# Down projections of an encoder trunk: the seven weight products interleaved, and a weight's three forms spread over three steps

## The chip, the cores and the metric

The kernel runs on one core of a Trainium2 chip, as one program and one launch. The metric is the device time of a whole execution in microseconds (us), lower is better; several executions are timed and the median counts. TensorE (PE) multiplies, VectorE (DVE), ScalarE (ACT) and GpSimd (POOL) do the element work, and SyncE (SP) and POOL start transfers from HBM into SBUF. PE's results go to PSUM.

## The reference

Two layers over 512 tokens of width 1024, in float32. Each layer has two feed-forward blocks (SwiGLU, hidden width 2816) with attention between them and a small embedding gate behind them:

```python
def swiglu(x, w_gate, w_up, w_down):
    return (jax.nn.silu(x @ w_gate) * (x @ w_up)) @ w_down
...
h += 0.5 * SwiGLU_1(RMSNorm(h))
...
h += 0.5 * SwiGLU_2(RMSNorm(h))
```

So there are four feed-forward blocks, and the change is in the last product of each, `@ w_down`: 512 tokens x 2816 times 2816 x 1024.

## The kernel before

*Number format.* PE multiplies float32 as split numbers: each operand is cut into a high part (a copy on ACT, L148, in `split`) and a low part (source minus high part, on DVE, L149), and every product is three matmuls, high x high, high x low, low x high. In `product` these are the lines L452, L453 and L454.

*Feed-forward block* (`ffn`). A loop over 22 pairs of hidden chunks computes gate and up projections (`pair_front`, `pair`, `pair_fast`) and leaves the activations a[0] to a[21], 128 hidden rows by 512 tokens each. Then `down` computes the projection.

*Down projection* (`down`). It is a 2 x 2 block product with seven products in place of eight (a Strassen-Winograd form). Hidden rows are halved, a[k] and a[K2 + k] with K2 = 11; tokens are halved, `l` and `r`; the weight has the four quarters b11, b12, b21 and b22, 11 chunks of 128 x 512 each. A *unit* is two chunks of a quarter, 128 x 1024 or 512 KB; there are six units, the last of one chunk. The seven products accumulate in PSUM over the six units and use these weights and activations:

| product | weight | activation | PSUM |
|---|---|---|---|
| r1, first half | b11 | x1, left | mm |
| r3, first half | b11 + b12 | x1, right | sc |
| r2 | b21 | x2, left | mm, ob |
| rb | b12 + b22 | x3, left | tr |
| r1, second half | b12 + b22 + b11 | x3, right | mm |
| rc | b12 + b22 + b11 + b21 | x2, right | mm, ob |
| r3, second half | b22 | x4 | sc |

x1 to x4 are the split parts of a[k] or a[K2 + k] after subtractions and additions on POOL (L467, L489, L490, L492). x1 takes the right half of a[k] less that of a[K2 + k].

*Weights.* `load` (L439) brings a unit by SP's queue into one of five raw buffers `wr`. `add` (L443) lays another quarter's unit onto the same buffer by an accumulating transfer on POOL's queue. `parts` splits the buffer into `wh` (ACT) and `wl` (DVE), of which there are four each. A raw buffer thus goes through as many as four forms; an add may start only when the split of the form before it has read the buffer, and the next split only when the add has landed.

*Order.* The statements are written out product by product. A scheduler reorders them somewhat before the program is fixed; after that each engine takes its instructions in a fixed order, and each queue its transfers. In the kernel before there are three loops over the units (called loop 1, 2 and 3 below), then r3's second half (a fourth), in which the x4 parts are made, and a tail: transposes on PE (L520), then 0.5 times the result plus the stream `kept` (L524), the next norm's scaling and split (`norm_split`, L211 and L212) and its squares (L224).

Of the kernel before, what the change touches and what calls it, by code (L numbers as in the profile page):

```python
# [20 lines left out]
NF = DFF // P  # L21
# [15 lines left out]
K2 = NF // 2  # L37
# [9 lines left out]
class Trunk:  # L47
# [353 lines left out]
    def ffn(self, i, which, k_next):  # L401


        nc, io = self.nc, self.io
        gu, dn = io[f"gu{which}"], io[f"dn{which}"]
        first = i == 0 and which == 1
        a, y, t = [], [None] * KC, [None] * (KC // 2)

        kept = io["xT"].rearrange("p c t -> c p t") if first else self.put_away()
        for m in range(NF):  # L410
# [11 lines left out]
        self.down(dn[i], a, kept)  # L422

    def down(self, w, a, kept):

        nc, H = self.nc, T // 2
        l, r = slice(0, H), slice(H, T)
        self.kept = self.dp.tile([KC, P, T], F32, name=self.nm("kept"))  # L430
        copy, tt, sub = nc.scalar.activation, nc.vector.tensor_tensor, ALU.subtract
        pool = nc.gpsimd.tensor_tensor
        b11, b12, b21, b22 = (w[n] for n in range(4))
        units = [slice(u, min(u + 2, K2)) for u in range(0, K2, 2)]
        ks = lambda u: range(u.start, u.stop)

        def load(b, u):
            raw = self.wr.tile([P, UNIT], F32, tag="wr", name=self.nm("wr"))[:, :(u.stop - u.start) * T]
            nc.sync.dma_start(raw, b[:, u.start * T:u.stop * T])  # L439
            return raw  # L440

        def add(raw, b, u):
            nc.gpsimd.dma_start(raw, b[:, u.start * T:u.stop * T], accum_op=ALU.add)  # L443

        def product(out, u, ws, xs, cols, start, stop):
            mm = nc.tensor.matmul
            for j, k in enumerate(ks(u)):
                wh, wl = (x[:, j * T:(j + 1) * T] for x in ws)
                for i, p in enumerate(out):
                    c = slice(cols.start + i * P, cols.start + (i + 1) * P)  # L450
                    xh, xl = (x[:, c] for x in xs[k])
                    mm(p, xh, wh, start=start and k == 0, stop=False, skip_group_check=True)  # L452
                    mm(p, xh, wl, start=False, stop=False, skip_group_check=True)  # L453
                    mm(p, xl, wh, start=False, stop=stop and k == K2 - 1, skip_group_check=True)  # L454
# [8 lines left out]
        x1, x2, x3, x4 = ([None] * K2 for _ in range(4))  # L463
        for u in units:
            raw = load(b11, u)
            for k in ks(u):
                pool(a[k][:, r], a[k][:, r], a[K2 + k][:, r], op=sub)  # L467
# [12 lines left out]
        for o, p in zip(c1, r2):  # L480
            tt(o, p, o, op=ALU.add)
        c11 = c1

        rb, rc = [self.tbank(), self.tbank()], [self.bank(), self.obank()]
        for u in units:
            raw = load(b12, u)
            add(raw, b22, u)
            for k in ks(u):
                pool(a[k][:, r], a[k][:, r], a[k][:, l], op=sub)  # L489
                pool(a[k][:, l], a[k][:, r], a[K2 + k][:, r], op=ALU.add)  # L490
                x3[k] = self.split_chunk(a[k], nc.vector)
                pool(a[K2 + k][:, l], a[K2 + k][:, l], a[k][:, r], op=ALU.add)  # L492
            product(rb, u, self.parts(raw), x3, l, True, True)
            add(raw, b11, u)
            product(r1, u, self.parts(raw), x3, r, False, True)
            add(raw, b21, u)
            product(rc, u, self.parts(raw), x2, r, True, True)
        c2, c21 = copied(r1), [self.act(), self.act()]
        u3 = [self.act(), self.act()]
        for i in range(2):  # L500
            tt(u3[i], c2[i], rb[i], op=sub)
            tt(c21[i], rc[i], u3[i], op=ALU.add)
            tt(c5[i], c5[i], u3[i], op=sub)
        c22 = c5

        hs = []
        for m in range(KC):
            hs.append(self.act())
            nc.sync.dma_start(hs[m], kept[m])
        for u in units:  # L510
            raw = load(b22, u)
            for k in ks(u):
                hi, lo = self.act(F32R), self.act(F32R)
                self.split(a[K2 + k][:, l], hi[:, l], lo[:, l])
                x4[k] = hi, lo
            product(r3, u, self.parts(raw), x4, l, False, True)

        def turned(out, x, j):
            for i, y in enumerate(x):
                nc.tensor.transpose(out[:, i * P:(i + 1) * P], y[:, j * P:(j + 1) * P], self.ident)  # L520

        def done(m, p, c):
            h = hs[m]
            nc.vector.scalar_tensor_tensor(h[:, c], p, 0.5, h[:, c], op0=ALU.mult, op1=ALU.add)  # L524
# [942 lines left out]
```

## Time and profile before

| | us |
|---|---|
| median of 3 runs (lowest to highest) | 2456.99 (2453.18 to 2458.53) |
| profiled execution, its own time | 2457.63 |
| its span in the trace | 2455.9 |
| PE busy in the span | 2155.1 (88%) |
| DVE, ACT, POOL busy | 1627.9, 1130.8, 487.0 |
| DMA traffic | 339.09 MB, mean 138 GB/s |
| mean granted TensorE clock | 0.932 |

The profile divides the span in 40 slices and shows busy shares of them, groups instructions by line, engine and operation, and names for each group what ended the engine's idle time before it (its releaser). The trace behind it holds every instruction with start and length, which can be listed by engine (a timeline), by source line or by window of time. "DMA share" is the mean busy share of the core's 16 DMA engines. The four down projections begin at 238.1, 982.8, 1488.6 and 2162.8 us.

### The profile page before, as it was taken

The numbers are of one execution on the slowest core, as the hardware profiler recorded it, in microseconds if no ns is written. First come the engines' busy times: TensorE is split into PE (matmuls) and PEld (weight loads), VectorE is DVE, ScalarE is ACT, GpSimd is POOL, SyncE is SP. The second block draws the span as 40 slices with busy tenths as digits, with TensorE's granted clock in tenths as the row PEclk, the third lists the DMA queues.
The fourth block names the chain that finished last, engine by engine and source line by source line (L and its number), as shares of the span: only waits on it lengthen the run. The fifth ranks groups of instructions, "written<-read, shape, count | busy, mean of one in ns | idle before, by whom it ended". The sixth has DMA issues, their size and how long they took to land. (4 is left out here: it accounts for less than half of the span.)

```text
span 2455.9 us, 32981 instructions
## 1 busy us (share of the span) xinstructions
PE 2155.1 (88%) x12294; PEld 1839.0 (75%) x12294; DVE 1627.9 (66%) x2571; ACT 1130.8 (46%) x1902; POOL 487.0 (20%) x534
## 2 busy tenths in 40 slices
PE   9999766899999999676899997767999999976678
PEld 7999444778788999454689995445988899964456
DVE  8788442789767788452777885517777678855175
ACT  5455322467654455231554553414666545534142
POOL 0012320342211011330210114302000101143021
PEclk9999887999999999888899998878999999988789
DMA  6675464554335565474545764646442456646452
GB/s 198 176 184 144 107 133 93 196 97 94 91 87 163 152 181 162 93 150 77 201 146 151 188 173 92 152 85 188 121 112 83 155 158 181 172 88 148 85 185 77
DMA packets 128048, 339.09 MB, mean 138 GB/s; under 512 B 23824, under 2 KB 31504, under 8 KB 127888
## 3 DMA queue, kind: packets, MB, share of 16 engines
q1 hardware_dynamic: 97728, 241.52, 30.6%
q0 software_dynamic: 30016, 95.44, 22.7%
q8 instruction: 96, 1.57, 0.3%
q14 instruction: 64, 0.52, 0.1%
q10 hardware_dynamic: 144, 0.04, 0.0%
HBM read 308.62 MB, written 17.27 MB: 133 GB/s over the span
## 5 line engine op out<-in xcount | busy, mean ns | idle before, releaser
L149 DVE TENSOR_TENSOR wl<-wr,wh 128x1024 fp32r<-128x1024 f32 (+1 forms) x503 | 611.2, 1222 | 504.9 <-ACT wh L148 503.9
L148 ACT ACTIVATE wh<-wr 128x1024 fp32r<-128x1024 f32 (+1 forms) x503 | 511.6, 1028 | 833.6 <-DMA wr<-in_dn_dram 472.2
L372 PE MATMUL mm<-act,wh 128*128 128x256 f32 x1088 | 307.9, 283 | 0.0
L373 PE MATMUL mm<-act,wl 128*128 128x256 f32 x1088 | 307.9, 283 | 0.0
L371 PE MATMUL mm<-act,wh 128*128 128x256 f32 x1088 | 307.9, 283 | 0.0
L173 PE MATMUL mm<-act,wh 128*128 128x512 f32 (+1 forms) x648 | 256.1, 397 | 4.2 <-DVE act L664 2.5
L174 PE MATMUL mm<-act,wh 128*128 128x512 f32 (+1 forms) x648 | 257.0, 397 | 2.5 <-DVE act L212 2.5
L175 PE MATMUL mm<-act,wl 128*128 128x512 f32 (+1 forms) x648 | 256.2, 395 | 3.3 <-DVE wl L149 3.3
L452 PE MATMUL mm<-wh,act 128*128 128x512 f32 x264 | 127.1, 506 | 141.2 <-ACT wh L148 136.2
L371 PEld LDWEIGHTS mm<-act,wh 128*128 128x128 f32 x1088 | 208.9, 192 | 0.2
L372 PEld LDWEIGHTS mm<-act,wh 128*128 128x128 f32 x1088 | 208.9, 192 | 0.2
L373 PEld LDWEIGHTS mm<-act,wl 128*128 128x128 f32 x1088 | 208.9, 192 | 0.0
L452 PEld LDWEIGHTS mm<-wh,act 128*128 128x128 f32 x264 | 58.4, 233 | 181.9 <-ACT wh L148 163.6
L149 DVE TENSOR_TENSOR act<-act,act 128x512 fp32r<-128x512 f32 (+1 forms) x192 | 180.5, 985 | 13.5 <-ACT act L148 13.4
L443 POOL DMA_DIRECT2D wr<-in_dn_dram x96 | 85.2, 888 | 477.5 <-DVE wl L149 449.3
L349 POOL DMA_DIRECT2D wr<-in_gu_dram x68 | 60.0, 882 | 494.6 <-DMA wr<-in_gu_dram 251.8
L371 PE MATMUL sc<-act,wh 128*128 128x256 f32 x544 | 154.0, 283 | 0.0
L372 PE MATMUL sc<-act,wh 128*128 128x256 f32 x544 | 154.0, 283 | 0.0
L373 PE MATMUL sc<-act,wl 128*128 128x256 f32 x544 | 154.0, 283 | 0.0
L174 PEld LDWEIGHTS mm<-act,wh 128*128 128x128 f32 x648 | 123.7, 191 | 27.9 <-DVE act L212 4.8
L173 PEld LDWEIGHTS mm<-act,wh 128*128 128x128 f32 x648 | 123.2, 190 | 27.8 <-issue 2.7
L175 PEld LDWEIGHTS mm<-act,wl 128*128 128x128 f32 x648 | 123.6, 191 | 27.1 <-DVE wl L149 4.7
(232 smaller groups left out, 4998.9 us busy)
## 6 DMA issues: line engine op xcount, KB each, us to landing
wr<-in_gu_dram SPq DMA_DIRECT2D x176, 512.0 KB, 4.4
wr<-in_dn_dram SPq DMA_DIRECT2D x80, 512.0 KB, 3.7
wr<-in_dn_dram POOLq DMA_DIRECT2D x80, 512.0 KB, 5.9
wr<-in_gu_dram POOLq DMA_DIRECT2D x68, 512.0 KB, 5.5
rb<-in_gu_dram SPq DMA_DIRECT2D x68, 256.0 KB, 2.6
act<-kept SPq DMA_DIRECT2D x56, 256.0 KB, 5.3
wr<-in_qk_ab_dram SPq DMA_DIRECT2D x20, 512.0 KB, 3.9
kept<-act POOLq DMA_DIRECT2D x32, 256.0 KB, 4.8
```

The source lines that it names most:

```text
L148: self.put(self.nc.scalar.activation(hi, src, AF.Copy))
L149: self.put((lo_eng or self.nc.vector).tensor_tensor(lo, src, hi.bitcast(F32), op=ALU.subtract))
L173: mm(out, stat[0], mov[0], start=start, stop=False)
L174: mm(out, stat[0], mov[1], start=False, stop=False)
L175: return mm(out, stat[1], mov[0], start=False, stop=stop)
L349: nc.gpsimd.dma_start(rs, w[:, :UNIT], accum_op=ALU.add)
L371: mm(out, w[0][:, c], xs[k][0][:, x], start=start and k == 0, stop=False, skip_group_check=True)
L372: mm(out, w[0][:, c], xs[k][1][:, x], start=False, stop=False, skip_group_check=True)
L373: mm(out, w[1][:, c], xs[k][0][:, x], start=False, stop=stop and k == half - 1, skip_group_check=True)
L443: nc.gpsimd.dma_start(raw, b[:, u.start * T:u.stop * T], accum_op=ALU.add)
L452: mm(p, xh, wh, start=start and k == 0, stop=False, skip_group_check=True)
```

## The change

All of the change is in `ffn` and `down`.

- Loops 1 and 2 become one (loop A): step s has r1 of unit s, the add of b12, r2 of unit s with a raw buffer of its own, and r3 of unit s - 1.
- Loop 3 becomes a loop B of eight steps: step s loads b12 and adds b22 for unit s + 1, then rb of unit s and the add of b11, r1 of unit s - 1 and the add of b21, rc of unit s - 2. The x4 parts of unit s - 2 are made there too, in halves of one tile, and no longer in the loop of r3's second half.
- The first two subtractions and splits of x1 are written ahead of the last gate and up pair (`lead_part`).

The number of matmuls, of splits and of transfers is the same.

```diff
         for m in range(NF):
+            if m == NF - 1:
+                for k in range(2):
+                    self.lead_part(x1, a, k)
...
+    def lead_part(self, x1, a, k):
+        if x1[k] is None:
+            right = slice(T // 2, T)
+            self.nc.gpsimd.tensor_tensor(a[k][:, right], a[k][:, right], a[K2 + k][:, right], op=ALU.subtract)
+            x1[k] = self.split_chunk(a[k], self.nc.vector)
...
-        for u in units:
-            raw = load(b11, u)
-            for k in ks(u):
-                pool(a[k][:, r], a[k][:, r], a[K2 + k][:, r], op=sub)
-                x1[k] = self.split_chunk(a[k], nc.vector)
-            product(r1, u, self.parts(raw), x1, l, True, True)
-            add(raw, b12, u)
-            product(r3, u, self.parts(raw), x1, r, True, True)
-        c1, c5 = copied(r1), copied(r3)
         r2 = [self.bank(), self.obank()]
-        for u in units:
-            raw = load(b21, u)
-            for k in ks(u):
-                x2[k] = self.split_chunk(a[K2 + k], nc.vector)
-            product(r2, u, self.parts(raw), x2, l, True, True)
+        n, raws = len(units), {}
+        for s in range(n + 1):
+            if s < n:
+                u = units[s]
+                raw = raws[s] = load(b11, u)
+                for k in ks(u):
+                    self.lead_part(x1, a, k)
+                product(r1, u, self.parts(raw), x1, l, True, True)
+                add(raw, b12, u)
+                raw = load(b21, u)
+                for k in ks(u):
+                    x2[k] = self.split_chunk(a[K2 + k], nc.vector)
+                product(r2, u, self.parts(raw), x2, l, True, True)
+            if s:
+                u = units[s - 1]
+                product(r3, u, self.parts(raws[s - 1]), x1, r, True, True)
+        c1 = copied(r1)
         for o, p in zip(c1, r2):
             tt(o, p, o, op=ALU.add)
-        c11 = c1
+        c11, c5 = c1, copied(r3)
+
+        def summed(s):
+            raws[s] = load(b12, units[s])
+            add(raws[s], b22, units[s])
 
         rb, rc = [self.tbank(), self.tbank()], [self.bank(), self.obank()]
-        for u in units:
-            raw = load(b12, u)
-            add(raw, b22, u)
-            for k in ks(u):
-                pool(a[k][:, r], a[k][:, r], a[k][:, l], op=sub)
-                pool(a[k][:, l], a[k][:, r], a[K2 + k][:, r], op=ALU.add)
-                x3[k] = self.split_chunk(a[k], nc.vector)
-                pool(a[K2 + k][:, l], a[K2 + k][:, l], a[k][:, r], op=ALU.add)
-            product(rb, u, self.parts(raw), x3, l, True, True)
-            add(raw, b11, u)
-            product(r1, u, self.parts(raw), x3, r, False, True)
-            add(raw, b21, u)
-            product(rc, u, self.parts(raw), x2, r, True, True)
+        summed(0)
+        for s in range(n + 2):
+            if s + 1 < n:
+                summed(s + 1)
+            if s < n:
+                u = units[s]
...
+                product(rb, u, self.parts(raws[s]), x3, l, True, True)
+                add(raws[s], b11, u)
+            if 0 < s <= n:
+                u = units[s - 1]
+                product(r1, u, self.parts(raws[s - 1]), x3, r, False, True)
+                add(raws[s - 1], b21, u)
+            if s > 1:
+                u = units[s - 2]
+                product(rc, u, self.parts(raws[s - 2]), x2, r, True, True)
+                for k in ks(u):
+                    t = self.act(F32R)
+                    x4[k] = t[:, l], t[:, r]
+                    self.split(a[K2 + k][:, l], *x4[k])
...
         for u in units:
             raw = load(b22, u)
-            for k in ks(u):
-                hi, lo = self.act(F32R), self.act(F32R)
-                self.split(a[K2 + k][:, l], hi[:, l], lo[:, l])
-                x4[k] = hi, lo
             product(r3, u, self.parts(raw), x4, l, False, True)
```

Three places show how instructions stand on the engines. In the rows, a name is a tile with its number; the part before the arrow is written, the part behind it read. The lines of the changed kernel are numbered anew: L450 is `load`, L454 `add`, L463 to L465 the matmuls of `product`, L545 the transposes, L549 the sums with the stream.

PE, behind r1's first unit, before (the tiles `mm` are r1's, the tiles `sc` r3's):

```order
L454 MATMUL mm_2759<-wh_2774,act_2771 128x512
L452 MATMUL sc_2760<-wh_2791,act_2765 128x512
L452 MATMUL sc_2761<-wh_2791,act_2765 128x512
L453 MATMUL sc_2760<-wl_2792,act_2765 128x512
L454 MATMUL sc_2760<-wh_2791,act_2766 128x512
```

The same place in the changed kernel (`mm_2772` and `ob_2773` are r2's):

```order
L465 MATMUL mm_2769<-wh_2776,act_2640 128x512
L463 MATMUL mm_2772<-wh_2803,act_2795 128x512
L464 MATMUL mm_2772<-wl_2804,act_2795 128x512
L465 MATMUL mm_2772<-wh_2803,act_2796 128x512
L463 MATMUL ob_2773<-wh_2803,act_2795 128x512
```

Where r3 of the same unit followed r1, r2 of that unit now follows, and then come r1 and r2 of the next unit and r3 of the first.

POOL's transfers in loop 3, before, from the add that is last of its kind ahead of the run of chained ones (a `wr` number names a raw buffer's unit: 3244, 3311, 3378, 3445 and 3512 are units 1 to 5):

```order
L443 DMA wr_3177<-in_dn_dram 128x1024
L443 DMA wr_3244<-in_dn_dram 128x1024
L443 DMA wr_3512<-in_dn_dram 128x512
L443 DMA wr_3244<-in_dn_dram 128x1024
L443 DMA wr_3311<-in_dn_dram 128x1024 x2
L443 DMA wr_3378<-in_dn_dram 128x1024 x2
L443 DMA wr_3445<-in_dn_dram 128x1024 x2
L443 DMA wr_3512<-in_dn_dram 128x512 x2
```

The same queue in loop B of the changed kernel (3177, 3180, 3214, 3265, 3338 and 3411 are units 0 to 5):

```order
L454 DMA wr_3177<-in_dn_dram 128x1024
L454 DMA wr_3180<-in_dn_dram 128x1024
L454 DMA wr_3338<-in_dn_dram 128x1024
L454 DMA wr_3177<-in_dn_dram 128x1024
L454 DMA wr_3214<-in_dn_dram 128x1024
L454 DMA wr_3180<-in_dn_dram 128x1024
L454 DMA wr_3265<-in_dn_dram 128x1024
L454 DMA wr_3411<-in_dn_dram 128x512
L454 DMA wr_3214<-in_dn_dram 128x1024
```

Two adds onto one unit stood next to each other; now those of two or three units alternate.

DVE at the end of the stage, before (L547 takes r3's second half, `sc`, out of PSUM):

```order
L212 SCALAR_TENSOR_TENSOR act_3764<-act_3572,gain,act_3763 128x512
L212 SCALAR_TENSOR_TENSOR act_3778<-act_3574,gain,act_3777 128x512
L149 TENSOR_TENSOR wl_3884<-wr_3882,wh_3883 128x1024
L547 TENSOR_TENSOR act_3554<-sc_2760,act_3554 128x256 x2
L547 TENSOR_TENSOR act_3555<-sc_2761,act_3555 128x256
```

The same place in the changed kernel (L572 takes r3's second half out of PSUM):

```order
L149 TENSOR_TENSOR wl_3873<-wr_3871,wh_3872 128x1024
L572 TENSOR_TENSOR act_3587<-sc_2770,act_3587 128x256 x2
L572 TENSOR_TENSOR act_3588<-sc_2771,act_3588 128x256
L549 SCALAR_TENSOR_TENSOR act_3601<-tr_3719,act_3601 128x512
L549 SCALAR_TENSOR_TENSOR act_3603<-tr_3732,act_3603 128x512
L572 TENSOR_TENSOR act_3588<-sc_2771,act_3588 128x256
L212 SCALAR_TENSOR_TENSOR act_3726<-act_3601,gain,act_3725 128x512
```

The four wide norm scalings of 128 x 512 (and the four sums that feed them) stood ahead of r3's last use; they now stand behind it.

More of the change, by code (lines that the diff above doesn't have):

```diff
@@ L409, in ffn @@
         kept = io["xT"].rearrange("p c t -> c p t") if first else self.put_away()
+        x1 = [None] * K2
         for m in range(NF):
+            if m == NF - 1:
+                for k in range(2):
+                    self.lead_part(x1, a, k)
             if m < FRONT:
@@ L421, in ffn, with down @@
         self.begin_norm(k_next)
-        self.down(dn[i], a, kept)
-    def down(self, w, a, kept):
+        self.down(dn[i], a, x1, kept)
+    def lead_part(self, x1, a, k):
[3 more added lines that the diff above has]
+            x1[k] = self.split_chunk(a[k], self.nc.vector)
+    def down(self, w, a, x1, kept):
         nc, H = self.nc, T // 2
@@ L462, in down @@
         r1, r3 = [self.bank(), self.bank()], [self.sbank(), self.sbank()]
-        x1, x2, x3, x4 = ([None] * K2 for _ in range(4))
-        for u in units:
-            raw = load(b11, u)
-            for k in ks(u):
-                pool(a[k][:, r], a[k][:, r], a[K2 + k][:, r], op=sub)
-                x1[k] = self.split_chunk(a[k], nc.vector)
-            product(r1, u, self.parts(raw), x1, l, True, True)
-            add(raw, b12, u)
-            product(r3, u, self.parts(raw), x1, r, True, True)
@@ L472, in down @@
-        c1, c5 = copied(r1), copied(r3)
-        r2 = [self.bank(), self.obank()]
-        for u in units:
-            raw = load(b21, u)
-            for k in ks(u):
-                x2[k] = self.split_chunk(a[K2 + k], nc.vector)
-            product(r2, u, self.parts(raw), x2, l, True, True)
+        r2 = [self.bank(), self.obank()]
+        x2, x3, x4 = ([None] * K2 for _ in range(3))
+        n, raws = len(units), {}
[14 more added lines that the diff above has]
+                product(r3, u, self.parts(raws[s - 1]), x1, r, True, True)
@@ new lines, in down @@
+        for s in range(n + 2):
[4 more added lines that the diff above has]
+                for k in ks(u):
+                    pool(a[k][:, r], a[k][:, r], a[k][:, l], op=sub)
+                    pool(a[k][:, l], a[k][:, r], a[K2 + k][:, r], op=ALU.add)
+                    x3[k] = self.split_chunk(a[k], nc.vector)
+                    pool(a[K2 + k][:, l], a[K2 + k][:, l], a[k][:, r], op=ALU.add)
+                product(rb, u, self.parts(raws[s]), x3, l, True, True)
[7 more added lines that the diff above has]
+                product(rc, u, self.parts(raws[s - 2]), x2, r, True, True)
+                for k in ks(u):
+                    t = self.act(F32R)
+                    x4[k] = t[:, l], t[:, r]
+                    self.split(a[K2 + k][:, l], *x4[k])
```

## The prediction, made before the changed kernel was run

> **What bounds the kernel now.** I read the page's costliest groups first, for the lines of the diff (a bracketed arrow names what ended an engine's idle time):
>
> ```profile
> L149 DVE TENSOR_TENSOR wl<-wr,wh 128x1024 fp32r<-128x1024 f32 (+1 forms) x503 | 611.2, 1222 | 504.9 <-ACT wh L148 503.9
> L148 ACT ACTIVATE wh<-wr 128x1024 fp32r<-128x1024 f32 (+1 forms) x503 | 511.6, 1028 | 833.6 <-DMA wr<-in_dn_dram 472.2
> L452 PE MATMUL mm<-wh,act 128*128 128x512 f32 x264 | 127.1, 506 | 141.2 <-ACT wh L148 136.2
> L443 POOL DMA_DIRECT2D wr<-in_dn_dram x96 | 85.2, 888 | 477.5 <-DVE wl L149 449.3
> ```
>
> The down projections' matmuls (L452) wait for the weight's high part (ACT), ACT waits for the weight's transfer, and the accumulating transfer (POOL, L443) waits for the low part (DVE): a ring. The windows of the four stages, first r1 matmul to last r3 matmul (length, then busy time of PE, weight load, DVE, ACT, POOL; granted clock; DMA share; GB/s):
>
> ```profile
> 238.10:451.20 213.10, 149.40 (x485) 106.55 (x484) 100.39 (x106) 67.91 (x97) 55.27 (x61) 0.81 0.55 126
> 982.80:1195.50 212.70, 146.92 (x485) 103.62 (x484) 101.08 (x106) 67.79 (x97) 55.80 (x61) 0.82 0.55 126
> 1488.60:1701.30 212.70, 147.51 (x486) 104.07 (x485) 100.33 (x107) 67.93 (x98) 55.34 (x61) 0.83 0.55 126
> 2162.80:2377.00 214.20, 147.89 (x485) 105.03 (x484) 97.82 (x106) 67.87 (x97) 55.23 (x61) 0.82 0.55 126
> ```
>
> They are alike, mean 213.2 us. No engine is full, DMA is at 0.55, and the clock falls to 0.82. Stage one by parts (loops 1 and 2; loop 3; the wait for r3):
>
> ```profile
> 238.00:322.00 84.00, 61.60 (x213) 43.55 (x211) 48.55 (x45) 30.36 (x44) 37.29 (x41) 0.88 0.57 128
> 322.00:425.40 103.40, 66.30 (x188) 46.08 (x188) 29.70 (x32) 23.33 (x28) 12.09 (x15) 0.76 0.47 88
> 425.40:434.20 8.80, 4.60 (x19) 3.13 (x18) 7.71 (x10) 3.23 (x6) 2.16 (x3) 0.50 0.94 308
> ```
>
> The ring in loop 3, on the timelines of POOL and ACT (start, length):
>
> ```profile
> 338.33 0.87 POOL L443 DMA_DIRECT2D wr<-in_dn_dram  x1 [8.48 <-DVE wl L149]
> ...
> 346.54 0.87 POOL L443 DMA_DIRECT2D wr<-in_dn_dram  x1 [5.50 <-DVE wl L149]
> 355.97 0.87 POOL L443 DMA_DIRECT2D wr<-in_dn_dram  x1 [8.57 <-DVE wl L149]
> ```
> ```profile
> 343.93 1.06 ACT L148 ACTIVATE wh<-wr 128x1024 fp32r<-128x1024 f32 x1 [7.34 <-DMA wr<-in_dn_dram]
> 352.23 2.00 ACT L148 ACTIVATE wh<-wr 128x1024 fp32r<-128x1024 f32 x2 [7.25 <-DMA wr<-in_dn_dram]
> ```
>
> One add of the chain every 8.8 us (338.33 to 355.97, halved; the row left out is a unit's first add, fetched ahead): issue, landing and split in a row. Two such adds make a unit, hence some 17.6 us for 36 matmuls.
>
> What PE needs alone, from the last r3 matmuls of stage one:
>
> ```profile
> 447.62 0.39 PE L452 MATMUL sc<-wh,act 128*128 128x512 f32 x1
> ...
> 450.80 0.39 PE L454 MATMUL sc<-wh,act 128*128 128x512 f32 x1
> ```
>
> 15 matmuls start 3.18 us apart from first to last, 0.227 us each: 462 of a stage are 105 us. So 108 us of each stage are waits and cold clock; that is the pot.
>
> **The change part by part.** It adds no matmul, split or transfer; it changes which waits overlap.
>
> *Loop A (r1, r2, r3 interleaved), 198 matmuls, PE floor 45 us.* Between r1(s) and r3(s), which is the add b12's round trip of 8.8 us, PE now has r2(s), r3(s-1), r1(s+1) and r2(s+1): 48 matmuls or 10.9 us. So the trip is covered. DVE and POOL then decide:
>
> ```profile
> 233.00:252.00 19.00, 16.59 (x80) 13.59 (x79) 16.45 (x17) 8.80 (x16) 18.20 (x17) 0.82 0.27 55
> ```
> ```profile
> L467 POOL TENSOR_TENSOR act<-act,act 128x256 f32<-128x256 f32 x44 | 32.2, 733 | 257.9 <-DVE act L398 257.9
> L489 POOL TENSOR_TENSOR act<-act 128x256 f32<-128x256 f32 x44 | 48.7, 1140 | 9.6 <-DVE act L149 9.6
> ```
> ```profile
> 232.64 0.69 DVE L149 TENSOR_TENSOR act<-act,act 128x512 fp32r<-128x512 f32 x1
> ```
> ```profile
> L149 DVE TENSOR_TENSOR act<-act,act 128x512 fp32r<-128x512 f32 x30 | 33.5, 1163 | 2.5 <-ACT act L148 2.5
> ```
>
> In a quiet place a chunk's low part takes 0.69 us on DVE and a POOL operation 0.73; side by side (the mean of stage one, the mean of L489) 1.16 and 1.14. A pair takes 1.17 us where one after the other would be 1.42: side by side is 1.21 times as fast as in turn. Loop A's DVE work: three products' weights, 3 x (5 x 1.22 + 0.69) = 20.4, and 31 chunk parts (9 of x1, 11 of x2, 11 of x3, which run early as in the kernel before) x 0.69 = 21.4, together 41.8. POOL: two late subtractions and 22 for x3, 24 x 0.73 = 17.5. (41.8 + 17.5) / 1.21 = 49 us. ACT has at most 39 splits x 1.03 = 40. I take **49** for loop A; ends 45 (PE alone) and 59 (DVE and POOL strictly in turn). Before: 84.
>
> The Trainium skill ("SBUF — State Buffer", section "SBUF: two separate sides") says that VectorE and GpSimd share a port pair under an exclusive lock, held for a whole instruction, so the loser stands still. It would give the 59; the trace does not bear it out strictly, since 0.69 + 0.73 in turn is more than the 1.17 seen.
>
> *Between the loops.* r1, r2 and r3 end together; the copies of r3 and their POOL and DVE followers hold ACT. Before, the same spot cost:
>
> ```profile
> 327.47 0.80 PE L452 MATMUL mm<-wh,act 128*128 128x512 f32 x1 [5.83 <-ACT wh L148]
> ```
>
> That gap held a whole add, which now is issued one unit ahead. I take **3 + 2** (ends 0 and 5.8): 3 wait, 2 for the cold clock behind it, by these rows:
>
> ```profile
> 268.37 0.73 PE L452 MATMUL sc<-wh,act 128*128 128x512 f32 x2 [1.61 <-ACT wh L148]
> ...
> 269.89 0.39 PE L453 MATMUL sc<-wl,act 128*128 128x512 f32 x1
> ```
> ```profile
> 400.21 1.06 PE L452 MATMUL mm<-wh,act 128*128 128x512 f32 x2 [2.51 <-ACT wh L148]
> ...
> 402.06 0.63 PE L454 MATMUL mm<-wh,act 128*128 128x512 f32 x1
> ```
>
> 1.61 us idle left the matmuls at 0.39 us, 2.51 us left them at 0.63; a dozen cold ones cost about 2 us more. The Trainium skill ("TensorE: Matmul & The Clock Gate", section on HAM oscillation) sets the harmful gap above about 3.4 us; by it the 2 would drop out, 8 us over four stages, but the row at 400.21 speaks against it.
>
> *Loop B (rb of s, r1 of s-1, rc of s-2), 198 matmuls, PE floor 45.* Each add now waits for a split of its own step and is used a step later; between rb(s) and r1(s) PE has 36 matmuls, 8.2 us, against the trip of 8.8. Three adds and one load per step are in flight. Then the 16 DMA engines count. Loop 3's transfers over 98 us (322 to 420):
>
> ```profile
> q0 software_dynamic: 1910, 6.35, 39.5%
> q1 hardware_dynamic: 720, 2.36, 8.3%
> ...
> wr<-in_dn_dram POOLq DMA_DIRECT2D x9, 512.0 KB, 5.6
> ```
>
> Accumulating: 0.395 x 98 / 6.35 = 6.1 us of all engines per MB; plain: 0.083 x 98 / 2.36 = 3.45. Loop B has 18 adds of 8.65 MB and six loads of 2.88 MB: 52.8 + 9.9 = 62.7 us. About 12 us of that (three loads at 1.8, two adds at 3.2) fit into loop A, whose own need is 17.6 for adds and 11 loads less five fetched before the stage, 10.9, or 28.5 of 49 us. 62.7 - 12 + 3 for the last split and its matmuls: **54** (ends 48, PE with its drain, and 66, no head start). That the adds can lie side by side is seen in loop 2 of the kernel before:
>
> ```profile
> 305.44 0.88 POOL L443 DMA_DIRECT2D wr<-in_dn_dram  x1
> ...
> 307.82 0.88 POOL L443 DMA_DIRECT2D wr<-in_dn_dram  x1
> ...
> 310.64 0.88 POOL L443 DMA_DIRECT2D wr<-in_dn_dram  x1 [1.10 <-DVE act L149]
> ```
> ```profile
> 300.00:322.00 22.00, 18.48 (x72) 12.59 (x71) 20.40 (x20) 11.65 (x19) 13.41 (x15) 1.00 0.89 220
> ```
>
> Adds 2.4 and 2.8 us apart, the engines at 0.89. Before: 103.4. The x4 splits now sit in this loop, where ACT and DVE had most of their time idle: no cost (11 x 0.69 = 7.6 us at most, if each delayed a weight).
>
> *r3's second half*, 66 matmuls: **15** (17 with a cold start). Transposes and stream loads that came between (8.8 us, above) now come behind or beside it.
>
> *Tail.* That has a price. Before, the first four chunks' sums (L524) and norms (L212) were over before r3 ended at 451.2:
>
> ```profile
> 430.97 1.34 DVE L524 SCALAR_TENSOR_TENSOR act<-tr,act 128x512 f32<-128x512 f32 x2 [0.38 <-DMA act<-in_xT_dram]
> ```
> ```profile
> 443.70 1.41 DVE L212 SCALAR_TENSOR_TENSOR act<-act,gain,act 128x512 fp32r<-128x512 f32 x2
> ...
> 446.71 1.41 DVE L212 SCALAR_TENSOR_TENSOR act<-act,gain,act 128x512 fp32r<-128x512 f32 x2
> ```
>
> Now all transposes stand behind r3 in PE's order, and 4 x 0.67 + 4 x 0.71 = 5.5 us of DVE follow it, partly under other waits: **5** (ends 2 and 6).
>
> *First parts ahead of the last pair:* two splits, which DVE did inside that pair before as well (232.64): nothing; if PE waited for them, 2 x 0.69 us.
>
> Sum: 49 + 5 + 54 + 15 + 5 = 128 us against 213.2, that is 85 less, times four 341. The profiled execution took 2457.63 (span 2455.9), against a median of 2456.99; 2457.6 - 341 = **2117 us**.
>
> **The rivals.** (1) *DMA as the bound*: no head start in loop B, 66 instead of 54: 2165. For it: 0.89 share in loop 2. Against: 0.55 over the stage. (2) *DVE and POOL in turn* through loop A, 59 or 60: 2159. (3) Both: 2207. (4) *Adds only in pairs*: 9 rounds of 8.8 us and 3 is 82 for loop B, 2229; for it ACT takes splits in order, so a late landing holds the next two. (5) *The other side*: each add still waits for the one before it, since POOL and ACT both take their work in a fixed order. 18 adds x 8.8 = 158 us for loop B, stage 232, 19 more than now: 2533. It turns where an add costs over 7.7 us in series ((213.2 - 74) / 18). Against it are the adds 2.4 us apart. (6) PE's wait merely moves, and nothing is gained.
>
> **How the numbers follow.** Forecast 0.55, (1) 0.17, (2) 0.12, (3) 0.05, (4) 0.05, (5) 0.04, (6) 0.02. If every term falls at its lower end: 45 + 0 + 48 + 15 + 2 = 110, 2045. The range runs from a little above that, 2055, to 2205, holding the forecast, (1) and (2) and leaving (3) to (6) out. A difference within 0.2% could not be told from none here. Faster 0.94, same 0.02, slower 0.04.
>
> **What would show it.** In the new profile: r1, r2, r3 over within 45 to 60 us of a stage's start; POOL's adds in loop B about 3 us apart rather than 8.8; DMA share there above 0.8; granted clock of the stage above 0.95; matmuls waiting for the high part for under 30 us in all instead of 136; L549 and L212 all behind r3. Wrong would be adds still 8 us apart, or a matmul gap at every step.

## The result, and the profile after

The changed kernel takes 2139.85 us (median of 4 runs, 2138.97 to 2141.0) against 2455.35 for the kernel before (four runs now, one more than ahead of the prediction): a ratio of 0.8714, 95% interval 0.8699 to 0.8730. The forecast was 2117 with a range of 2055 to 2205. The profiled execution took 2138.97 (span 2137.2, granted clock 0.981 where it was 0.932).

The four stages in the new trace, again from the first r1 matmul to the last r3 matmul (start:end, length, busy time of PE, weight load, DVE, ACT, POOL; clock; DMA share; GB/s):

```profile
238.70:364.90 126.20, 113.46 (x466) 89.47 (x465) 89.31 (x96) 62.19 (x90) 56.17 (x52) 0.95 0.84 203
900.30:1027.40 127.10, 111.57 (x466) 88.56 (x465) 89.63 (x96) 62.03 (x89) 56.16 (x52) 0.96 0.83 203
1327.70:1454.30 126.60, 113.38 (x466) 89.45 (x465) 88.32 (x94) 61.47 (x89) 56.16 (x52) 0.95 0.83 199
1922.90:2051.00 128.10, 113.47 (x466) 89.95 (x465) 89.81 (x96) 62.18 (x89) 56.21 (x52) 0.93 0.83 201
```

They take 127.0 us in the mean where they took 213.2; over the four stages that is about 345 us less. The span fell by 318.7 only, so 26 us came back outside the stages. The groups by line say what became of the ring:

```profile
L148 ACT ACTIVATE wh<-wr 128x1024 fp32r<-128x1024 f32 (+1 forms) x503 | 516.0, 1029 | 577.7 <-DMA wr<-in_dn_dram 148.5
```
```profile
L454 POOL DMA_DIRECT2D wr<-in_dn_dram x96 | 83.8, 901 | 185.1 <-DVE wl L149 122.2 <-DMA wr<-in_dn_dram 60.5 <-issue 2.4
L463 PE MATMUL sc<-wh,act 128*128 128x512 f32 x176 | 70.9, 403 | 18.9 <-ACT wh L148 18.9
L463 PE MATMUL mm<-wh,act 128*128 128x512 f32 x264 | 103.7, 393 | 0.0
L463 PE MATMUL tr<-wh,act 128*128 128x512 f32 x88 | 40.9, 465 | 17.1 <-ACT act L148 17.1
```

ACT's wait for down weights fell from 472 us to 148, POOL's wait in front of the adds from 477 to 185, and the wait of the first matmuls of a product for a weight's high part from 136 us on `mm` alone to 18.9, all on `sc`. On `tr` (rb's tiles) a new wait of 17.1 us stands, for the high part of an activation. POOL's timeline in loop B of stage one shows the adds (start, length):

```profile
306.37 0.87 POOL L454 DMA_DIRECT2D wr<-in_dn_dram  x1 [3.74 <-DVE wl L149]
308.11 0.87 POOL L454 DMA_DIRECT2D wr<-in_dn_dram  x1 [0.87 <-DVE wl L149]
309.85 0.87 POOL L454 DMA_DIRECT2D wr<-in_dn_dram  x1 [0.87 <-DVE wl L149]
317.12 0.87 POOL L454 DMA_DIRECT2D wr<-in_dn_dram  x1 [6.41 <-DVE wl L149]
319.56 1.76 POOL L454 DMA_DIRECT2D wr<-in_dn_dram  x2 [1.58 <-DMA wr<-in_dn_dram]
323.99 0.87 POOL L454 DMA_DIRECT2D wr<-in_dn_dram  x1 [2.66 <-DVE wl L149]
```

They go out 2.9 us apart in this piece (306.37 to 323.99 is six intervals), where one in 8.8 us had been; with 7.0 us to landing in the median (last section) two to three are in flight. Stage one by parts (loop A but for r3's last six matmuls; the turn and the start of loop B; the rest of loop B; r3's second half), same columns as above (the DMA share adds up the times of packets, so it can pass 1):

```profile
238.70:289.20 50.50, 45.48 (x194) 35.38 (x192) 44.11 (x37) 23.30 (x33) 43.16 (x37) 1.00 0.66 162
289.20:312.00 22.80, 15.09 (x38) 10.34 (x39) 11.45 (x14) 10.61 (x16) 6.06 (x7) 0.70 1.04 210
312.00:349.70 37.70, 37.70 (x168) 31.21 (x167) 24.56 (x34) 22.31 (x34) 6.96 (x8) 1.00 0.90 197
349.70:364.90 15.20, 15.20 (x69) 12.55 (x68) 9.20 (x12) 5.96 (x7) 0.00 (x0) 1.00 0.95 342
```

Loop A runs at full clock with short waits. The second row is where the stage still loses: PE has 15.1 us of work in 22.8, at a clock of 0.70. From 312 on PE never stops. ACT's longest wait stands there, for the add of b12 onto the last unit of loop A, without whose split r3's last matmuls can't start:

```profile
292.53 0.63 ACT L148 ACTIVATE wh<-wr 128x512 fp32r<-128x512 f32 x1 [10.12 <-DMA wr<-in_dn_dram]
```

The table has the parts' lengths of this trace and of the experiments, in us, mean of the four stages, from the start times of the matmuls: loop A to its 192nd matmul; from there to rb's first matmul (the turn, with r3's last six matmuls in it; in the kernels with loops 1 and 2, r2's last six); to r3's second half; r3's second half. "Outside" is the span less the four stages. The parts come from one profiled execution each. Each ratio is to runs of the kernel before that were taken beside that kernel, with medians from 2455 to 2460, so kernels are compared by their ratios.

| kernel | loop A | turn | loop B | r3 | outside | median | ratio to the kernel before (95%) |
|---|---|---|---|---|---|---|---|
| before | 80.0 | 1.2 | 115.2 | 16.7 | 1603.3 | 2455.35 | 1 |
| the change | 50.5 | 9.2 | 52.2 | 15.1 | 1629.2 | 2139.85 | 0.8714 (0.8699 to 0.8730) |
| loop A alone | 50.5 | 9.3 | 114.1 | 16.5 | 1605.7 | 2367.74 | 0.9625 (0.9607 to 0.9644) |
| loop B alone | 79.2 | 1.4 | 54.8 | 15.1 | 1632.2 | 2236.55 | 0.9094 (0.9077 to 0.9111) |
| two stages a step | 50.5 | 9.3 | 75.5 | 15.8 | 1634.2 | 2241.53 | 0.9113 (0.9096 to 0.9130) |
| half adds | 50.5 | 8.4 | 50.2 | 15.1 | 1628.1 | 2123.7 | 0.8635 (0.8618 to 0.8651) |
| b12 first | 50.5 | 8.9 | 51.1 | 15.1 | 1627.9 | 2133.61 | 0.8681 (0.8666 to 0.8697) |
| x3 first | 50.5 | 9.2 | 50.7 | 15.1 | 1629.1 | 2136.75 | 0.8692 (0.8675 to 0.8709) |
| tail between | 50.5 | 9.5 | 52.1 | 16.6 | 1602.1 | 2115.48 | 0.8610 (0.8594 to 0.8626) |
| no POOL work | 43.7 | 4.1 | 54.2 | 15.1 | 1625.6 | 2098.82 | 0.8543 (0.8524 to 0.8562) |
| three mends | 50.5 | 8.6 | 50.6 | 16.6 | 1605.1 | 2112.96 | 0.8598 (0.8586 to 0.8609) |
| POOL work late | 43.7 | 5.2 | 57.7 | 16.6 | 1607.5 | 2099.56 | 0.8544 (0.8531 to 0.8556) |
| x4 back | 50.5 | 9.3 | 61.6 | 17.1 | 1599.1 | 2146.79 | 0.8734 (0.8721 to 0.8746) |
| no first parts | 50.3 | 10.0 | 52.0 | 15.1 | 1626.3 | 2140.69 | 0.8711 (0.8699 to 0.8723) |

### The profile page after: what moved, and what is told of

Its sections match the earlier page's. It is cut to its first block, busy times and chain, and to the rows that moved or that the text cites. A ratio compares the mean times of both kernels' runs of the same rounds, so it can differ in the third digit from the quotient of the medians.

```text
span 2137.2 us, 33010 instructions
## 1 busy us (share of the span) xinstructions
PE 2032.2 (95%) x12294; PEld 1785.7 (84%) x12294; DVE 1620.7 (76%) x2571; ACT 1131.5 (53%) x1902; POOL 526.1 (25%) x534
## 4 chain that ended last, share of the span: by engine, by line
PE 69%; DVE 10%; DMA 7%; issue 6%; POOL 4%; ACT 3%; SPq 0%; DVEq 0%; POOLq 0%; ACTq 0%
PE mm L373 6%; PE mm L372 6%; PE mm L371 6%; PE mm L174 6%; PE mm L173 6%; PE mm L175 6%; DMA wr<-in_dn_dram 5%; DVE wl L149 3%; PE sc L373 3%; PE sc L372 3%; PE sc L371 3%; PE sc L173 2%; PE sc L175 2%; PE sc L174 2%; DVE act L212 1%
## 5 line engine op out<-in xcount | busy, mean ns | idle before, releaser
L149 DVE TENSOR_TENSOR wl<-wr,wh 128x1024 fp32r<-128x1024 f32 (+1 forms) x503 | 632.7, 1262 | 223.0 <-ACT wh L148 219.8
L149 DVE TENSOR_TENSOR act<-act,act 128x512 fp32r<-128x512 f32 (+1 forms) x192 | 150.7, 817 | 4.2 <-ACT act L148 4.1
L224 POOL TENSOR_TENSOR ssq<-ssq,tmp 128x512 f32<-128x512 f32 x48 | 70.1, 1460 | 324.0 <-ACT tmp L217 323.3
L454 POOL DMA_DIRECT2D wr<-in_dn_dram x96 | 83.8, 901 | 185.1 <-DVE wl L149 122.2
L464 PE MATMUL mm<-wl,act 128*128 128x512 f32 x264 | 104.7, 397 | 14.0 <-DVE wl L149 14.0
```

The source lines that it names most:

```text
L149: self.put((lo_eng or self.nc.vector).tensor_tensor(lo, src, hi.bitcast(F32), op=ALU.subtract))
L224: self.last_sum = eng.tensor_tensor(self.acc, self.acc, sq, op=ALU.add)
```

## The experiments

**Loop A alone, loop B alone.** The first keeps the new loop A and the old loop 3 (with x4 split in r3's loop); the second the old loops 1 and 2 and the new loop B. In both the first parts stay.

```diff
 # loop A alone
-        for s in range(n + 2):
...
+        for u in units:
+            raw = load(b12, u)
+            add(raw, b22, u)
...
+            add(raw, b11, u)
+            product(r1, u, self.parts(raw), x3, r, False, True)
+            add(raw, b21, u)
+            product(rc, u, self.parts(raw), x2, r, True, True)
```

> Only loop A and the first parts are taken over; loop 3, the x4 splits and r3's second half are as in the kernel before. Theory (each loop's own ring was the loss): loop A with its turn falls from about 81 to about 59 us a stage, loop 3 stays near 103 and the tail as it was, so 4 x 22 = 88 us less, about 2368 us. Rival (the gain comes from the two loops together, transfers of loop 3 being fetched under loop A): under 60 us less, above 2395.

> Only loop B, with the x4 splits in it, and the first parts; loops 1 and 2 are as in the kernel before. Theory: r1 to r2 keep their 81 us, loop B takes 52 to 58 and the 8.7 us ahead of r3 go, the tail costs 6 to 7: 4 x 55 = 220 less, about 2235 us, and with the run of loop A alone the two gains add up to the 315 of the whole change within 15 us. Rival (loop B needs the head start from loop A's idle transfers): loop B takes 63 or more and the gain is under 190, above 2265.

Measured: 0.0375 and 0.0906 of the time of before, together 0.1281, where the whole change saves 0.1286. The two gains add up, and both medians lie close to the theory's; each loop had its own ring. Loop B takes 54.8 us behind the old loops and 52.2 behind the new one, so it hardly needs loop A's idle transfers. A head start it had in both: three adds or more go out in the 15 us ahead of rb's first matmul.

**Two stages a step.** rc of a unit in the step of its r1:

```diff
-        for s in range(n + 2):
+        for s in range(n + 1):
...
-            if s > 1:
-                u = units[s - 2]
-                product(rc, u, self.parts(raws[s - 2]), x2, r, True, True)
+            if s:
+                u = units[s - 1]
+                product(rc, u, self.parts(raws[s - 1]), x2, r, True, True)
```

> The changed kernel with rc of a unit in the same step as its r1, so that loop B has two stages in place of three and the second add of a unit is not put a step away from its use. Theory (a step apart is what hides the add): each step has one open trip of an add, 8.8 us at the least and 10 to 11 under load, so loop B takes 57 to 65 us in place of 52, 20 to 52 us more than the changed kernel, 2160 to 2192 us. Rival (loop B is set by the transfers' total alone): within 8 us of the changed kernel, 2132 to 2148.

Measured: 75.5 us for loop B, 23 more than with three stages, and about 100 us in all. The sign is the theory's, the size twice the upper end of its forecast: 2241.5 for 2160 to 2192. POOL's timeline in that loop shows why:

```profile
327.86 0.86 POOL L454 DMA_DIRECT2D wr<-in_dn_dram  x1 [8.94 <-DVE wl L149]
329.00 0.86 POOL L454 DMA_DIRECT2D wr<-in_dn_dram  x1 [0.27 <-DVE wl L149]
341.31 0.86 POOL L454 DMA_DIRECT2D wr<-in_dn_dram  x1 [11.45 <-DVE wl L149]
342.44 0.86 POOL L454 DMA_DIRECT2D wr<-in_dn_dram  x1 [0.27 <-DVE wl L149]
353.79 0.86 POOL L454 DMA_DIRECT2D wr<-in_dn_dram  x1 [10.48 <-DVE wl L149]
```

Adds go out in pairs, 1.1 us apart, and then POOL waits 9 to 11 us: the step is 13 us (327.86 to 341.31 is 13.5, to 353.79 another 12.5). The first of a pair lands 5 to 6 us after its issue and the second some 8 us, and both must land before the next pair. That is the prediction's rival (4), adds only in pairs at 82 us a loop; the step of distance for the second add is what the change needs to escape it.

**Half adds.** It leaves out half of the bytes of the 18 adds of loop B (the first half of each unit's columns is added).

```diff
-            add(raws[s], b22, units[s])
+            half(raws[s], b22, units[s])
...
+        def half(raw, b, u):
+            w = (u.stop - u.start) * T // 2
+            nc.gpsimd.dma_start(raw[:, :w], b[:, u.start * T:u.start * T + w], accum_op=ALU.add)
```

> Leaves out half of the bytes of the 18 accumulating transfers of loop B (each lays only the first half of a unit's columns). Theory (in loop B the transfer engines are the bound, share 0.95): loop B falls from 52 to about 46, near TensorE's 45, and the gap ahead of it by 2 to 4: 4 x 8 to 10 = 32 to 40 us less than the changed kernel, about 2104 us. Rival (order of splits on ScalarE and VectorE sets loop B): under 10 us less, above 2130.

Measured: 19 us less than the change by the ratios (0.0079 of 2456; 12.5 between the two traces), half of what the theory said and twice what the rival allowed. Its window for the same piece of loop B:

```profile
312.00:346.50 34.50, 34.50 (x154) 28.58 (x153) 22.61 (x31) 18.99 (x29) 6.94 (x8) 1.00 0.65 141
```

DMA share is 0.65 in place of 0.90 and PE is as full as before. So from 312 us on PE is the bound, not the transfers. They matter in the first steps only: loop B is 2.0 us shorter, the turn 0.8.

**POOL beside VectorE.** It leaves out the 33 POOL operations that make x3 and x4 out of the activations.

```diff
-                    pool(a[k][:, r], a[k][:, r], a[k][:, l], op=sub)
-                    pool(a[k][:, l], a[k][:, r], a[K2 + k][:, r], op=ALU.add)
                     x3[k] = self.split_chunk(a[k], nc.vector)
-                    pool(a[K2 + k][:, l], a[K2 + k][:, l], a[k][:, r], op=ALU.add)
```

> Leaves out the 33 POOL operations that make x3 and x4 (these are then split from what stands in the activations). Theory (VectorE and POOL side by side stretch each other and set loop A): the four waits of 0.95 to 1.4 us for VectorE's low parts go, loop A falls from 50.5 to about 46, 16 to 24 us less than 2140. Rival (the order of splits alone sets loop A): under 6 us less.

Measured: 42 us less than the change (0.0171 of 2456), about twice what the theory said: loop A fell further than foreseen, and the turn got shorter too. Loop A takes 43.7 us, which is 192 matmuls at 0.2277: the floor. DVE's groups in loop A, of the change and then without POOL's work (count, busy us, mean ns, idle before):

```profile
L149 DVE TENSOR_TENSOR wl<-wr,wh 128x1024 fp32r<-128x1024 f32 x13 | 21.6, 1666 | 0.9 <-ACT wh L148 0.9
L149 DVE TENSOR_TENSOR act<-act,act 128x512 fp32r<-128x512 f32 x19 | 21.2, 1145 | 0.0
```
```profile
L149 DVE TENSOR_TENSOR wl<-wr,wh 128x1024 fp32r<-128x1024 f32 x14 | 17.2, 1227 | 6.3 <-ACT wh L148 6.3
L149 DVE TENSOR_TENSOR act<-act,act 128x512 fp32r<-128x512 f32 x18 | 11.7, 683 | 0.0
```

And POOL's in loop A of the change:

```profile
L513 POOL TENSOR_TENSOR act<-act,act 128x256 f32<-128x256 f32 x10 | 13.7, 1385 | 1.4 <-ACT act L148 0.7 <-DVE act L149 0.7
L511 POOL TENSOR_TENSOR act<-act,act 128x256 f32<-128x256 f32 x9 | 11.4, 1270 | 0.6
L510 POOL TENSOR_TENSOR act<-act 128x256 f32<-128x256 f32 x9 | 11.3, 1265 | 0.6 <-DVE act L149 0.6
```

POOL's operations take 1.27 to 1.39 us in place of 0.73, DVE's 1.67 and 1.15 in place of 1.23 and 0.68. It costs 6.8 us of loop A and 5 at the turn; loop B gives 2 back.

**Mends at the turn.** In the change, the add of b12 for loop A's last unit stands in POOL's queue behind the first add of b22, which waits for its load. "b12 first" turns the two round. "x3 first" puts the x3 high parts of unit 1 ahead of a weight split in ACT's order.

```diff
 # b12 first
+                last = add(raw, b12, u)
...
+        with self.tc.issue_after(last.ins):
+            summed(0)
 # x3 first
+                with self.tc.issue_after(third.ins) if s == 1 else ExitStack():
+                    ws = self.parts(raws[s - 1])
```

> The changed kernel with POOL's queue mended at the turn: the add of b12 onto loop A's last unit goes ahead of the first add of b22 for loop B, behind whose load it had waited. Theory (that queue place causes the 4.0 to 5.2 us gap ahead of r3's last six matmuls): the gap falls below 1.5 us and TensorE stays warm there, 3 to 4 us less per stage, 12 to 16 us less than the changed kernel, about 2126 us. Rival (the transfer engines are full from 281 to 312 us, so the wait only moves to rb's first unit): the gap shifts, and the time stays within 5 us of 2140.

> The changed kernel with ScalarE's queue mended at the turn: the x3 high parts of unit 1 go ahead of the split for r1's unit 0, which waits for a transfer. Theory (rb's second unit waits only for this place in ScalarE's order): the gap of 2.3 to 4.5 us ahead of rb's second unit goes, but r1's unit 0 still waits for its transfer, so 1 to 2.5 us less per stage, 4 to 10 us less than 2140. Rival (the wait only moves on to r1's unit 0): within 3 us of 2140.

Measured: 8 and 5 us less than the change by the ratios, 6 and 3 by the medians. The interval of "b12 first" lies just below the change's; its gain falls between its theory and its rival. That of "x3 first" overlaps the change's, so its gain is not shown, though in its trace the wait ahead of rb's second unit is gone and loop B is 1.5 us shorter, as its theory had it. PE's waits at the turn of stage one, of the change and of "b12 first":

```profile
293.21 0.63 PE L463 MATMUL sc<-wh,act 128*128 128x512 f32 x1 [4.04 <-ACT wh L148]
...
297.64 0.80 PE L463 MATMUL tr<-wh,act 128*128 128x512 f32 x1 [1.21 <-ACT act L148]
...
305.39 0.50 PE L463 MATMUL tr<-wh,act 128*128 128x512 f32 x1 [2.26 <-ACT act L148]
```
```profile
298.09 0.79 PE L463 MATMUL tr<-wh,act 128*128 128x512 f32 x1 [7.89 <-ACT act L148]
...
304.84 0.51 PE L463 MATMUL tr<-wh,act 128*128 128x512 f32 x1 [1.27 <-ACT act L148]
```

The 4.0 us ahead of r3's last unit are gone and stand, grown to 7.9, ahead of rb's first, which comes at 298 either way: as to the place of the wait, the rival's case. ACT's timeline in "b12 first" shows what rb's first unit waits for:

```profile
292.16 1.06 ACT L148 ACTIVATE wh<-wr 128x1024 fp32r<-128x1024 f32 x1 [3.20 <-DMA wr<-in_dn_dram]
295.49 1.06 ACT L148 ACTIVATE wh<-wr 128x1024 fp32r<-128x1024 f32 x1 [2.27 <-DMA wr<-in_dn_dram]
296.45 1.06 ACT L470 ACTIVATE act<-sc 128x512 f32<-128x512 f32 x2
297.41 1.15 ACT L148 ACTIVATE act<-act 128x512 fp32r<-128x512 f32 x2
```

ACT waits for two transfers and splits the weights of rb's first and second unit, copies r3's first half, and only then takes the high parts of x3 for which rb's first matmuls wait. So two things hold rb: the transfers, which are slow there (DMA share 1.04), and the place of these high parts in ACT's order, behind a split that only rb's second unit needs. How much each costs is open: no run put them ahead of that split, and half the bytes in loop B's adds made the turn only 0.8 us shorter.

**The tail between r3's units.** The transposes, sums and norms of the first four chunks are written behind r3's units 2 to 5, one each.

```diff
+        for j, u in enumerate(units):
             raw = load(b22, u)
             product(r3, u, self.parts(raw), x4, l, False, True)
+            m = j - 2
+            if 0 <= m < M:
+                p = self.tbank()
+                turned(p[:, l], c11, m)
+                turned(p[:, r], c21, m)
+                done(m, p, slice(0, T))
...
```

> The changed kernel with the transposes, stream sums and norms of the first four chunks written between r3's last units instead of behind r3. Theory (that work, 5.5 us of VectorE, is what the tail lost): each tail gets 3 to 5 us shorter, 12 to 20 us less than 2140. Rival (the loads of the stream land too late, since the transfer engines are at 0.93 from 349 to 365 us, and hold VectorE and with it r3's weights): r3 gets longer by as much, within 5 us of 2140 or slower.

Measured: 25 us less than the change (0.0104 of 2456), more than expected. Time outside the stages goes back to what it was before the change (1602 against 1603), and r3 pays 1.5 us a stage for it.

**The x4 splits back in r3's loop**, as before the change (the four added lines of the diff go back to where the three removed ones were).

> The changed kernel with the x4 splits back in the loop of r3's second half, in full tiles; by the order of instructions the transposes then stand ahead of r3 again. Theory (the tail's loss is that order, and the wait ahead of r3 its other side): 8.7 us of wait ahead of r3 and 1.7 in it come back, 6.8 us of tail go: 3.6 a stage, 14 us more than the changed kernel, about 2154. Rival (where the x4 splits stand makes no difference): within 4 us of 2140.

Measured: 0.8734 (0.8721 to 0.8746), some 5 us slower than the change where 14 were expected; the intervals touch. In its profiled execution, the slowest of its five runs (2155.2), the parts went as the theory said (loop B with the wait ahead of r3 9.4 longer, r3 2 longer, outside 7.5 shorter a stage). PE's order there is the old one, with its waits:

```profile
354.11 0.44 PE L545 MATMUL tr<-ident,act 128*128 128x128 f32 x2 [1.19 <-DVE act L527]
356.78 1.11 PE L545 MATMUL tr<-ident,act 128*128 128x128 f32 x4 [2.23 <-DVE act L549]
```

So where the x4 splits stand decides, by way of the scheduler, whether the transposes wait ahead of r3 or trail behind it; in this trace the one costs 11.4 us a stage and the other 7.5.

**No first parts** ahead of the last pair (the three lines in `ffn` left out).

> The changed kernel without the first parts ahead of the last pair. Theory (they are two splits that the scheduler would have put inside that pair anyway): loop A the same or up to 1.4 us longer and the pair up to 0.6 shorter, within 4 us of 2140. Rival (they are what lets loop A start without waits): loop A 3 us or more longer, above 2150.

Measured: 2140.69, ratio 0.8711: no difference, as the theory said. This part of the change does nothing that can be seen.

**Together, and POOL's work later.** "Three mends" is the tail between r3's units with both mends at the turn. "POOL work late" adds to it that POOL's operations for x3 of units 2 to 5 go behind that unit's add of b22, and those for x4 behind the add of b11:

```diff
+                    with self.tc.issue_after(raws[s, 0].ins) if s >= 2 else ExitStack():
+                        pool(a[k][:, r], a[k][:, r], a[k][:, l], op=sub)
+                        pool(a[k][:, l], a[k][:, r], a[K2 + k][:, r], op=ALU.add)
...
+                with self.tc.issue_after(add(raws[s], b11, u).ins):
+                    for k in ks(u):
+                        pool(a[K2 + k][:, l], a[K2 + k][:, l], a[k][:, r], op=ALU.add)
```

> The changed kernel with the three mends together: transposes and norms of four chunks between r3's units, b12's last add ahead of b22's first, x3's parts of unit 1 ahead of r1's split. Theory (they act at different places): 24 + 6 + 3 us less than the changed kernel's 2140, about 2107 us. Rival (the two at the turn only move the same wait): 2113 or above.

> As the run with the three mends, and POOL's operations for x3 of units 2 to 5 and all of its additions for x4 put behind adds of loop B in POOL's queue. Theory (loop A loses 6.8 us to POOL working beside VectorE, as leaving those operations out showed, and VectorE and POOL have idle time in loop B): loop A falls from 50.5 to 44 to 46, loop B stays within 1.5 us, 16 to 24 us less than the run with the three mends. Rival (the operations delay the adds of loop B, which stand behind them in the queue): loop B longer by 4 us or more, no gain in all.

Measured: 2112.96, some 3 us less than the tail's alone, with intervals that overlap; that is at the border of the rival, 2113. With POOL's work late 2099.56, 0.8544 of the kernel before and the fastest version here that computes everything: 13 us less than the three mends, where 16 to 24 were expected. Loop A is at its floor of 43.7 us, as the theory had it, and the turn 3.4 shorter, but loop B 7.1 longer, as the rival had it. The windows of 288 to 300 and 312 to 344 us in its first stage:

```profile
288.00:300.00 12.00, 5.05 (x13) 3.85 (x13) 12.00 (x6) 4.30 (x7) 11.92 (x13) 0.50 0.86 162
...
312.00:344.00 32.00, 30.97 (x134) 24.61 (x133) 22.67 (x24) 15.13 (x23) 11.85 (x14) 1.00 0.86 177
```
```profile
295.13 1.22 PE L465 MATMUL tr<-wh,act 128*128 128x512 f32 x2 [6.95 <-DVE act L149]
```

VectorE and POOL now meet at the turn: both are full for 12 us, VectorE does six operations in it, and rb waits 6.95 us for a low part. From 312 on the same POOL work does no harm. A version that keeps POOL's work out of the turn as well was not tried.

## Why the prediction was right, point by point

The time lies in the range, 22 us above the forecast, and the mechanism, the ring and its removal, is the one foretold. Of the terms of the sum, loop A and loop B came out near their sizes for other reasons than those given, and the turn was missed.

- *The ring is the loss, and distance removes it*: shown. Each loop's part alone gives its share, the shares add up to 0.1281 of 0.1286, and with the second add's distance taken away loop B goes from 52 to 75 us.
- *Loop A, 49*: 51.9 (50.5 and 1.4 for r3's last six matmuls). The mechanism, VectorE and POOL side by side, is shown by the run without POOL's work and by the one that moves this work out of loop A: 43.7 us in both. Two errors cancelled in the working. 31 chunk parts were counted, but the rows hold 19 act parts in loop A, since x3's parts mostly ran later (of POOL's operations it was the other way, 29 for 24). And side by side was taken to be 1.21 times as fast as in turn, from means that mix meetings with quiet spells. The rows above give DVE 13 x 1.23 + 19 x 0.68 = 28.9 us, with some 3 us of smaller work 32, and POOL 29 x 0.73 = 21, together 53 in turn, done in 50.5: 1.05 times as fast. That is close to rival (2)'s mechanism, with less work in it than rival (2) had. The Trainium skill ("SBUF — State Buffer", section "SBUF: two separate sides") with its exclusive lock describes this better than the prediction allowed, if not to the last: by the lock alone it would be the 53.
- *Turn, 3 + 2*: the term that failed most clearly, beyond its upper end of 5.8. It measured 7.8 (9.2 less the 1.4 of the six matmuls), and the cold clock reaches on into loop B: 0.70 over 289 to 312 us. The step that failed is that the add which the old gap held would now be out of the way: ACT waited 10.1 us for the one of loop A's last unit. The prediction had a wait only for the copies on ACT; the trace of stage one shows 4.0, 1.2 and 2.3 us of waits, while the transfer engines are at 1.04, and matmuls of 0.63 us between them.
- *Loop B, 54*: 52.2, but for another reason. It was put down to 62.7 us of transfers less a head start. The run with half the bytes took 50.2, and in stage one PE ran without a gap from 312 us. Loop B is PE's 45 and about 7 us of waits and cold clock at its start; the transfers' sum fitted by chance.
- *r3, 15*: 15.1. *Tail, 5*: 6.5 (1629.2 - 1603.3 over four), somewhat over its upper end of 6, and the run with the tail between r3's units shows its cause to be the order named.
- *First parts, nothing*: shown. *x4 splits in loop B, no cost*: right by itself, but they are what lets r3 start at once and so sends the transposes behind it; the prediction had seen the order and not its cause.
- *Signs foretold*: r1, r2 and r3 were over 57.8 us after the stage's start (45 to 60 foretold), the adds 2.9 us apart (3), the DMA share in loop B 0.90 and above (0.8), the clock of the stages 0.93 to 0.96 (above 0.95, met by one stage of four), the waits for the weights' high part 18.9 us (under 30; the 17.1 us for the activations' had not been foreseen), and L549 and L212 stood behind r3.
- Sum: 51.9 + 7.8 + 52.2 + 15.1 + 6.5 = 133.5 a stage against 128 forecast: loop A, turn and tail are 2.9, 2.8 and 1.5 over, loop B 1.8 under. Times four that is the 22 us by which 2117 was short.
- Rival (5), adds in series, did not come: adds lay 2.9 us apart. Nor did rival (1), loop B at 66 us by its transfers. That they are not its bound is shown by the run with half the bytes; what loop B would take without any head start was not tried, since loop B alone (54.8) had one too.

## What to carry to other kernels

When a buffer is transformed in several steps by different engines and queues, look for the ring in the waits (each names the next), and give every step a whole round of independent work before its result is used; doing so for all but one step, as in the run with two stages, gave back 23 of the 63 us that loop B had gained. Then sum each loop's floor for the busiest engine and look where the stage starts and turns: that is where the rest was, as waits that one engine hands to the next and as cold clock, and moving one transfer ahead there mostly moved the wait. An average over operations that sometimes meet another engine's and sometimes don't is no price for a loop where they always meet.

## What the runs showed of the hardware

- POOL's element operations and VectorE's two-input ones hardly overlap when both have work nearly all the time: 53 us of work in turn took 50.5 in loop A, and in the turn of the run with POOL's work late six VectorE operations took 12 us beside a full POOL.
- Accumulating transfers of 512 KB land in 7.0 us in the median in loop B of the change, with two or three in flight, and in 5.6 in loop 3 of the kernel before, where one of the chain went out every 8.8 us. The three of that size that the change issues at the turn, from 281 to 287 us, took 10.0. Loop B of the change moved 7.75 MB of them in 76.2% of 56 us:

```profile
q0 software_dynamic: 2357, 7.75, 76.2%
...
wr<-in_dn_dram POOLq DMA_DIRECT2D x11, 512.0 KB, 7.0
```

That is 5.5 us of all engines per MB, where 6.1 was worked out from the sparse loop 3: a price taken from a loop that waits was a tenth too high for one that doesn't.

- The length of a gap alone does not say whether PE's clock falls. In the kernel before, a gap of 1.93 us was followed, some 1.6 us later, by matmuls of 0.63 us for about 3 us, and one of 3.14 us by matmuls of 0.40; ahead of both the matmuls had taken 0.39:

```profile
1538.93 0.73 PE L452 MATMUL sc<-wh,act 128*128 128x512 f32 x2 [1.93 <-ACT wh L148]
...
1540.56 0.63 PE L454 MATMUL sc<-wh,act 128*128 128x512 f32 x1
```
```profile
2221.16 0.73 PE L452 MATMUL sc<-wh,act 128*128 128x512 f32 x2 [3.14 <-ACT wh L148]
...
2222.46 0.40 PE L453 MATMUL sc<-wl,act 128*128 128x512 f32 x1
```

So the prediction's two rows, 1.61 us warm and 2.51 us cold, were no bound to go by. Nor do these rows bear out the 3.4 us of the Trainium skill ("TensorE: Matmul & The Clock Gate", section on HAM oscillation) as one. What else decides, such as where in time the gap falls, was not tried.
